# One accumulator per block product in the second feed-forward GEMM, combined once at its end

## Chip, cores and metric

The kernel runs on one core of one Trainium2 chip. The metric is device time in microseconds (us) of one execution. The kernel before has a median of 2658.47 us over 3 runs (2654.43 to 2660.08).

## What is computed

The reference is a chain of four layers in fp32 on 1024 tokens of width 1024: a retention layer, a latent-attention layer, a gated-linear-attention layer and a feed-forward layer with squared ReLU, then a final norm. The change lies in the last part only:

```
def sqrelu_mlp(h, w1, w2):
    return jnp.square(jax.nn.relu(h @ w1)) @ w2
...
        x = x + sqrelu_mlp(rms_norm(x, norm_ffn), w1, w2)
    return rms_norm(x, final_norm)
```

Here w1 is 1024 x 4096 (called FF1 below) and w2 is 4096 x 1024 (FF2).

## The kernel before, in words

All activations are kept transposed (features on the 128 partitions, tokens along the row) as tiles of 128 x 512 fp32: half h is tokens 0 to 511 or 512 to 1023. Every fp32 operand is split into two fp32r parts, a high part made by ScalarE (ACT, a copy) and a low part made by VectorE (DVE, source minus high part); a product is then three matmuls, high by high, high by low and low by high (`mm3`, lines 230 to 232).

The GEMMs are run as 2 x 2 block products in the seven-product form of Strassen and Winograd. The seven products are named 1 to 7 and always come in the order 1, 2, 6, 7, 5, 4, 3 (`FIRST + REST`). Operands of 1, 2 and 3 are blocks as they are; 4, 5, 6 and 7 take sums of blocks. The weight sums are made by GpSimd (POOL) in `W7.sums` (line 638), then split by ACT and DVE (`w_split`, lines 629 and 630). There is room for one set of split weights: a pair of weight tiles is filled again as soon as the two products that read it are done.

**FF1** is 16 jobs of 256 output rows. Each job has 7 products of 12 matmuls of 128 x 512. Class `Fresh` takes the products out of PSUM (line 550 on DVE) and combines them into the four blocks (m, h) of the job. `u_done` applies ReLU, the row norm (line 2096, DVE) and the square (line 2099, ACT) and stores the tile to DRAM: four stores a job.

**FF2** goes over the 32 tiles of 128 rows of u in groups, `FF2_GROUPS = (3, 3, 3, 3, 2, 2)`: a group of k has 2k of these tiles as its inner dimension. For the first five groups, `ff2_operands` loads the group's 4k tiles (2k for each half) from DRAM (tile name `uin`), and `Blocks.add` makes the four operand sums of each k (line 452, two on DVE and one on POOL, and line 463 on POOL) and splits all seven operands (lines 187 and 188). Then it goes over the four column slices s of w2: 7 products of 3k matmuls each, whose results class `Added` adds at once into the four output tiles of the slice, which hold the residual from the start:

```
        def m7(self, ps):
            self.direct(ps, (1, 1), (1, 0))
            self.later(self.two, (1, 0))
```

`direct` is a DVE add from PSUM into the output tile (line 588), `plus` a DVE add of a product to a running sum u (line 597), `later` a POOL add of such a sum into an output tile (line 593). In a slice of a group that makes 7 DVE adds, one ACT copy and 4 POOL adds. The operands of a group are given back product by product in slice s = 3, and only then is there room for the next group's.

The last group (`ff_last`) is run as a plain product, 96 matmuls of 128 x 512 for half 0 and 192 of 128 x 256 for half 1, with the final norm folded in.

SBUF tiles of 128 x 512 come from a pool `slots` whose places are handed out oldest first. PSUM has 8 banks for products, taken in turn. Loads, weights and, at this stage, stores are all issued from SP's queue (lines 119, 122 and 686). The order of the instructions on each engine is set when the program is built: the writing order of the code with some parts marked as of high priority, then arranged by the framework's own timeline.

Of the kernel before, what the change touches and what calls it, by code (L numbers as in the profile page):

```python
# [13 lines left out]
F32 = mybir.dt.float32  # L14
F32R = mybir.dt.float32r
MASK = mybir.dt.uint8
AF = mybir.ActivationFunctionType
ALU = mybir.AluOpType
# [4 lines left out]
P = 128  # L23
QS = lambda nc: (nc.scalar, nc.sync)
T = 1024
HALF = 512
D = 1024
# [11 lines left out]
C_WIDE = 2  # L39
C_WAIT = 16  # L40
C_LAST = 3
C_TAIL = "01 11 21- 02 A 12 22- w0 w1 A 06 B 07 A 05 B w0 w2 04 A 03 B 16 17 B w1 15 14 13 w2 26- 27- 25- a 24- a 23- b"
C_NORM = "NP"
C_DVE = 3
# [37 lines left out]
def tile_kernel(ctx, tc, a, out):  # L82
    nc = tc.nc
# [34 lines left out]
    def store(dst, src):  # L118
        store_q.dma_start(out=dst, in_=src)

    def load(dst, src):
        load_q.dma_start(out=dst, in_=src)
# [1964 lines left out]
    for _ in last:  # L2087
        pass
    x7 = nd.x7


    u_dram = {}

    def u_done(i, m, h, ts):
        (t,) = ts
        nc.vector.scalar_tensor_tensor(
            out=t, in0=t, scalar=0.0, in1=nd.rb[h], op0=ALU.max, op1=ALU.mult
        )
        nc.scalar.activation(out=t, in_=t, func=AF.Square)
        d = dp.tile([P, HALF], F32, name=f"u_{i}_{m}_{h}")  # L2100
        store(d, t)
        slots.put(t)
        u_dram[2 * i + m, h] = d

    def ff1_job(i, early=False):
        w = W7(a["w_ff1"][i], w7p)
# [18 lines left out]

    hd = {}

    def ff2_operands(k, j):
        u7 = Blocks(slots, k)
        for h in range(2):  # L2130
            for i in range(2 * k):
                t = slots.get("uin")
                load(t, u_dram[j + i, h])
                u7.add(i, h, t)
        return u7

    j = 0
    for g, k in enumerate(FF2_GROUPS[:-1]):
        u7 = ff2_operands(k, j)
        j += 2 * k  # L2140
        for s in range(4):
            if g == 0:
                slots.held.update(NORM_TAGS)
                for m, h in ((1, 0), (0, 0), (1, 1), (0, 1)):
                    hd[2 * s + m, h] = slots.get(f"y{2 * s + m}_{h}")
                    load(hd[2 * s + m, h], nd.dram[2 * s + m, h])
                slots.held.clear()
            w = W7(a[f"w_ff2_{g}"][s], w7p)
            w.rest()
            drop = u7.drop if s == 3 else None  # L2150
            Added(plain_product, hd, 2 * s).run(w.w, u7.x, FIRST + REST, drop)

    def ff_last(g, k):
        slots.held.update(NORM_TAGS)
        u = {}
        for h in range(2):
            for i in range(2 * k):
                t = slots.get("uin")
                load(t, u_dram[j + i, h])
                u[i, h] = slots.get("uh", F32R), slots.get("ul", F32R)  # L2160
                split(*u[i, h], t)
                slots.put(t)

        def tiles(w, s, h, cols, norm):
            wh, wl = w
            for m2 in range(2):
                m = 2 * s + m2
                ps = bank8()[:, : cols.stop - cols.start]
                for i in range(2 * k):
                    c = (((1, 0), (2, 3))[m2][i // k] * k + i % k) * P  # L2170
                    c = slice(c, c + P)
                    x = (t[:, cols] for t in u[i, h])
                    mm3(ps, wh[:, c], wl[:, c], *x, i == 0, i == 2 * k - 1)
                tick()
                o = hd[m, h][:, cols]
                with tc.high_priority():
                    nc.vector.tensor_tensor(out=o, in0=ps, in1=o, op=ALU.add)
                norm.add(o)
                g = gain("final_norm_2", m)
                nc.scalar.activation(out=o, in_=o, func=AF.Copy, scale=g)  # L2180

        def done(h, cols, norm, n):
            yield n
            r4 = norm.rstd(pc)
            yield n
            rb = spread(r4, pc, "rbp")
            for m in range(NK):
                o = hd[m, h][:, cols]
                eng = nc.gpsimd if n or m % 3 == 2 else nc.vector
                eng.tensor_tensor(out=o, in0=o, in1=rb, op=ALU.mult)  # L2190
                c = slice(h * HALF + cols.start, h * HALF + cols.stop)
                nc.sync.dma_start(out=out[m * P : (m + 1) * P, c], in_=o)

        ws = {}
        for h, cols in ((0, slice(0, HALF)), (1, slice(0, 256)), (1, slice(256, HALF))):
            last = cols.start > 0
            norm = NormOnTensor(D) if last else Norm(D, (nc.vector,))
            for s in range(4):
                if s not in ws:
                    ws[s] = load_w(a[f"w_ff2_{g}"][s])  # L2200
                tiles(ws[s], s, h, cols, norm)
            defer(done(h, cols, norm, 0 if last else 1))
# [77 lines left out]
def prepare(inp):  # L2280
# [63 lines left out]
    row = 0  # L2344
    for i, k in enumerate(FF2_GROUPS):
        rows = w2[row * P : (row + 2 * k) * P]
        r[f"w_ff2_{i}"] = np.stack([blocks(cut(rows, s, 256), 1) for s in range(4)])
        row += 2 * k
    return r
# [1 line left out]

# [14 lines left out]
```

## Time and profile before

| what | value |
|---|---|
| median of 3 runs | 2658.47 us |
| the profiled execution | 2656.4 us |
| its span, first to last instruction | 2654.6 us |
| mean granted TensorE clock | 0.965 of full speed |
| PE busy | 2480.7 us (93%) |
| DVE busy | 2043.8 us (77%) |
| ACT busy | 1094.7 us (41%) |
| POOL busy | 1322.9 us (50%) |
| DMA, all queues | 305.59 MB, mean 115 GB/s |

PE is TensorE's matmuls and PEld its weight loads; shares are of the span. Matmuls are pipelined, so a busy PE says little about how fast it goes: the number of matmuls in a stretch says more. [...]

### The profile page before, as it was taken

The numbers are of one execution on the slowest core, as the hardware profiler recorded it, in microseconds if no ns is written. First come the engines' busy times: TensorE is split into PE (matmuls) and PEld (weight loads), VectorE is DVE, ScalarE is ACT, GpSimd is POOL, SyncE is SP. The second block draws the span as 40 slices with busy tenths as digits, with TensorE's granted clock in tenths as the row PEclk, the third lists the DMA queues.
The fourth block names the chain that finished last, engine by engine and source line by source line (L and its number), as shares of the span: only waits on it lengthen the run. The fifth ranks groups of instructions, "written<-read, shape, count | busy, mean of one in ns | idle before, by whom it ended". The sixth has DMA issues, their size and how long they took to land. (4 is left out here: it accounts for less than half of the span.)

```text
span 2654.6 us, 35499 instructions
## 1 busy us (share of the span) xinstructions
PE 2480.7 (93%) x12676; PEld 2067.6 (78%) x12676; DVE 2043.8 (77%) x2967; ACT 1094.7 (41%) x1882; POOL 1322.9 (50%) x973
## 2 busy tenths in 40 slices
PE   7999999999997999999998988889999999988888
PEld 5888888877785788888877878777778888766767
DVE  8787787789978835767578677887796676898895
ACT  7323323354443324555444433334553333333334
POOL 4345444435736712222135266865453333888884
PEclk8999999999998999999997989989999999988999
DMA  6523223633333322122342333446333334523322
GB/s 228 161 78 117 105 91 119 211 105 110 105 114 116 101 90 75 58 63 73 120 136 81 109 122 108 138 159 216 123 115 113 106 102 136 162 81 95 91 91 81
DMA packets 141005, 305.59 MB, mean 115 GB/s; under 512 B 16123, under 2 KB 19579, under 8 KB 140828
## 3 DMA queue, kind: packets, MB, share of 16 engines
q1 hardware_dynamic: 118940, 263.47, 31.0%
q10 hardware_dynamic: 21888, 39.86, 4.0%
q8 instruction: 100, 1.64, 0.3%
q14 instruction: 77, 0.63, 0.1%
HBM read 213.08 MB, written 88.08 MB: 113 GB/s over the span
## 5 line engine op out<-in xcount | busy, mean ns | idle before, releaser
L593 POOL TENSOR_TENSOR y<-y,u 128x512 f32<-128x512 f32 x120 | 205.6, 1731 | 75.7 <-DVE y L588 37.2
L629 ACT ACTIVATE wh<-ws 128x1024 fp32r<-128x1024 f32 (+3 forms) x200 | 142.6, 725 | 201.5 <-PE ps L231 106.9
L630 DVE TENSOR_TENSOR wl<-ws,wh 128x1024 fp32r<-128x1024 f32 (+3 forms) x196 | 198.8, 1022 | 22.9 <-ACT wh L629 22.4
L638 POOL TENSOR_TENSOR wsb<-wsc 128x512 f32<-128x512 f32 (+2 forms) x72 | 103.1, 1433 | 218.4 <-issue 137.7
L629 ACT ACTIVATE wh<-wsb 128x1024 fp32r<-128x1024 f32 (+2 forms) x76 | 73.6, 968 | 214.8 <-PE ps L231 134.1
L1428 POOL TENSOR_SCALAR p<-p,rl 128x512 f32<-128x512 f32 (+2 forms) x96 | 61.2, 648 | 194.7 <-DVE rl L1426 93.5
L638 POOL TENSOR_TENSOR ws<-ws,wsb 128x512 f32<-128x512 f32 (+2 forms) x72 | 102.3, 1421 | 96.2 <-DVE wl L630 96.2
L550 DVE TENSOR_TENSOR y<-ps,one 128x512 f32<-128x512 f32 x108 | 73.5, 686 | 93.3 <-PE ps L232 43.8
L550 DVE TENSOR_TENSOR y<-ps,y 128x512 f32<-128x512 f32 x112 | 76.9, 686 | 76.4 <-PE ps L232 50.0
L638 POOL TENSOR_TENSOR wsb<-ws,wsb 128x512 f32<-128x512 f32 (+2 forms) x72 | 111.0, 1542 | 49.1 <-DMA ws<-w_a 40.9
L550 DVE TENSOR_TENSOR one<-ps,one 128x512 f32<-128x512 f32 x168 | 114.3, 683 | 21.0 <-PE ps L232 18.7
L588 DVE TENSOR_TENSOR y<-ps,y 128x512 f32<-128x512 f32 x152 | 99.8, 681 | 30.7 <-POOL y L593 25.7
L630 DVE TENSOR_TENSOR wl<-wsc,wh 128x1024 fp32r<-128x1024 f32 (+2 forms) x76 | 112.3, 1483 | 10.9 <-ACT wh L629 10.2
L231 PE MATMUL ps<-x5l,wh 128*128 128x512 f32 x248 | 101.6, 410 | 11.4 <-DVE x5l L188 8.4
L638 POOL TENSOR_TENSOR wsc<-wsc,ws 128x512 f32<-128x512 f32 (+2 forms) x72 | 111.8, 1553 | 0.0
L230 PE MATMUL ps<-x6h,wh 128*128 128x512 f32 x248 | 102.8, 417 | 7.4 <-ACT wh L629 4.1
L230 PE MATMUL ps<-x1h,wh 128*128 128x512 f32 x248 | 101.5, 410 | 8.7 <-ACT x1h L192 8.0
L230 PE MATMUL ps<-x3h,wh 128*128 128x512 f32 x248 | 102.1, 412 | 7.6 <-DVE y L588 7.6
L230 PE MATMUL ps<-x2h,wh 128*128 128x512 f32 x248 | 102.2, 413 | 5.7 <-ACT wh L629 4.4
L630 DVE TENSOR_TENSOR wl<-wsb,wh 128x1024 fp32r<-128x1024 f32 (+2 forms) x76 | 105.3, 1385 | 2.4 <-ACT wh L629 2.0
L232 PE MATMUL ps<-x5h,wl 128*128 128x512 f32 x248 | 101.2, 408 | 4.0 <-DVE wl L630 4.0
L231 PE MATMUL ps<-x6l,wh 128*128 128x512 f32 x248 | 101.5, 409 | 3.1 <-DVE x6l L188 3.1
(475 smaller groups left out, 8860.4 us busy)
## 6 DMA issues: line engine op xcount, KB each, us to landing
uin<-u SPq DMA_DIRECT2D x64, 256.0 KB, 3.5
u<-y SPq DMA_DIRECT2D x48, 256.0 KB, 2.0
ws<-w_ff SPq DMA_DIRECT2D x23, 512.0 KB, 4.5
ws<-w_a SPq DMA_DIRECT2D x21, 512.0 KB, 5.2
ws<-w_b SPq DMA_DIRECT2D x20, 512.0 KB, 3.3
wsc<-w_a SPq DMA_DIRECT2D x16, 512.0 KB, 4.4
v<-v SPq DMA_DIRECT2D x32, 256.0 KB, 3.6
gate<-g SPq DMA_DIRECT2D x32, 256.0 KB, 3.2
```

Source lines behind the costliest of these rows:

```text
L230: nc.tensor.matmul(ps, lh, rh, start=start, stop=False)
L231: nc.tensor.matmul(ps, lh, rl, start=False, stop=False)
L232: nc.tensor.matmul(ps, ll, rh, start=False, stop=stop)
L550: nc.vector.tensor_tensor(out=o, in0=p, in1=i, op=ALU.add)
L588: nc.vector.tensor_tensor(out=t, in0=ps[0], in1=t, op=ALU.add)
L593: nc.gpsimd.tensor_tensor(out=t, in0=t, in1=u, op=ALU.add)
L629: nc.scalar.activation(out=hi, in_=raw, func=AF.Copy)
L630: lo_eng.tensor_tensor(out=lo, in0=raw, in1=hi.bitcast(F32), op=ALU.subtract)
L638: eng.tensor_tensor(out=o, in0=x, in1=y, op=op)
L1428: nc.gpsimd.tensor_scalar(out=pr, in0=pr, scalar1=rl, scalar2=0.0, op0=ALU.mult, op1=ALU.add)
```

## The change

- In FF1, for the first 14 jobs, the four tiles of a job are kept until the last is squared. Then POOL makes the operand sums from them (`u_sums`, four adds), and seven tiles are stored instead of four. The last two jobs still store their four tiles.
- In FF2, `split_load` loads each of the seven operands of a k ready made, into the place of its low part, and splits it there: 7k loads for a group instead of 4k, and no sums.
- `Sevens` keeps, for each slice s, one SBUF accumulator for each of the seven products over all five groups (28 in all instead of 16 output tiles). A product is one DVE add from PSUM into its accumulator; accumulators 2, 4 and 3 start as residual tiles loaded from DRAM, the other four are filled by an ACT copy in the first group. There are no POOL adds until `close`, which follows each slice of the fifth group and does four adds on DVE and four on POOL.
- Seven more places in the pool (`f_slots`). The scratch for descriptors of DMAs issued from GpSimd is cut to 2048 bytes; this kernel issues none there.
- The rows of w2 are put in another order on the host, so that the pair of tiles of one FF1 job forms the two block rows.

```diff
+F_SLOTS = 7
...
+    fslots = pool(ctx, "f_slots")
+    slots.add(fslots, [f"f{i}" for i in range(F_SLOTS)])
...
+    def u_sums(i):
+        b11, b21, b12, b22 = (u_raw.pop((i, m, h)) for h in range(2) for m in range(2))
+        t1, n6 = slots.get("t1"), slots.get("n6")
+        G = nc.gpsimd
+        G.tensor_tensor(out=t1, in0=b12, in1=b11, op=ALU.subtract)
+        G.tensor_tensor(out=n6, in0=t1, in1=b22, op=ALU.subtract)
+        G.tensor_tensor(out=b12, in0=b12, in1=b22, op=ALU.subtract)
+        keep_u(6, i, n6)
+        G.tensor_tensor(out=n6, in0=b21, in1=n6, op=ALU.add)
+        for n, t in ((1, b11), (2, b21), (7, b12), (5, t1), (4, n6), (3, b22)):
+            keep_u(n, i, t)
+            slots.put(t)
+
+    def keep_u(n, i, t):
+        u_dram[n, i] = dp.tile([P, HALF], F32, name=f"u{n}_{i}")
+        store(u_dram[n, i], t)
...
         nc.scalar.activation(out=t, in_=t, func=AF.Square)
-        d = dp.tile([P, HALF], F32, name=f"u_{i}_{m}_{h}")
-        store(d, t)
-        slots.put(t)
-        u_dram[2 * i + m, h] = d
+        if i >= 16 - FF2_GROUPS[-1]:
+            keep_u((m, h), i, t)
+            slots.put(t)
+            return
+        u_raw[i, m, h] = t
+        if (m, h) == (0, 1):
+            u_sums(i)
...
-    def ff2_operands(k, j):
-        u7 = Blocks(slots, k)
-        for h in range(2):
-            for i in range(2 * k):
-                t = slots.get("uin")
-                load(t, u_dram[j + i, h])
-                u7.add(i, h, t)
-        return u7
+    def split_load(src):
+        lo, hi = slots.get("lo", F32R), slots.get("hi", F32R)
+        raw = lo.bitcast(F32)
+        load(raw, src)
+        split(hi, lo, raw)
+        return hi, lo
+
+    class Sevens:
+        OF = {2: (0, 0), 4: (1, 0), 3: (0, 1)}
...
+        def run(self, w, x, drop):
+            for n in FIRST + REST:
+                if n not in self.acc:
+                    slots.held.update(NORM_TAGS)
+                    self.acc[n] = self.old(*self.OF[n]) if n in self.OF else slots.get("y")
+                    slots.held.clear()
+                    first = n not in self.OF
+                else:
+                    first = False
+                (ps,) = plain_product(w[n], x[n])
+                t = self.acc[n]
+                with tc.high_priority():
+                    if first:
+                        nc.scalar.activation(out=t, in_=ps, func=AF.Copy)
+                    else:
+                        nc.vector.tensor_tensor(out=t, in0=ps, in1=t, op=ALU.add)
+                if drop:
+                    for pair in x[n]:
+                        slots.put(*pair)
+
+        def close(self):
+            a, V, G = self.acc, nc.vector, nc.gpsimd
+            last = self.old(1, 1)
+            for e, o, i in (
+                (V, 2, 1), (G, 6, 1), (V, 7, 6), (G, 6, 5), (V, 4, 7), (V, 5, 7), (G, 3, 6)
+            ):
+                e.tensor_tensor(out=a[o], in0=a[o], in1=a[i], op=ALU.add)
+            G.tensor_tensor(out=a[5], in0=a[5], in1=last, op=ALU.add)
...
+    ys = [Sevens(s) for s in range(4)]
     for g, k in enumerate(FF2_GROUPS[:-1]):
-        u7 = ff2_operands(k, j)
-        j += 2 * k
-        for s in range(4):
...
-            drop = u7.drop if s == 3 else None
-            Added(plain_product, hd, 2 * s).run(w.w, u7.x, FIRST + REST, drop)
+        x = {n: [split_load(u_dram[n, j + i]) for i in range(k)] for n in FIRST + REST}
+        j += k
+        for s, c in enumerate(ys):
+            w = W7(a[f"w_ff2_{g}"][s], w7p)
+            w.rest()
+            c.run(w.w, x, s == 3)
+            if g == len(FF2_GROUPS) - 2:
+                c.close()
...
+        if i < len(FF2_GROUPS) - 1:
+            rows = rows.reshape(k, 2, P, D).transpose(1, 0, 2, 3).reshape(-1, D)
...
-    nc = bacc.Bacc("TRN2", target_bir_lowering=False, num_devices=1)
+    nc = bacc.Bacc("TRN2", target_bir_lowering=False, num_devices=1, dynamic_dma_scratch_size=2048)
```

Ahead of FF1 no engine's order changes, and PE's order in FF1 stays as it was. Two places show what moves. Line numbers are each kernel's own: from line 42 on, those of the changed kernel stand one or more higher.

The first place is DVE at the change from the third group of FF2 to the fourth, in slice s = 3. Before (x5l, x3l, x6l are low parts of operands, uin the loaded tiles, wl low parts of weights, y and u the adds of products):

```order
L188 TENSOR_TENSOR x5l_22358<-uin,x5h_22357 128x512
L188 TENSOR_TENSOR x3l_22378<-uin,x3h_22377 128x512
L597 TENSOR_TENSOR u<-ps_22282,u 128x512
L452 TENSOR_TENSOR uin<-uin 128x512
L188 TENSOR_TENSOR x5l_22365<-uin,x5h_22364 128x512
L630 TENSOR_TENSOR wl<-wsb,wh 128x768
L188 TENSOR_TENSOR x3l_22399<-uin,x3h_22398 128x512
...
L188 TENSOR_TENSOR x5l_22372<-uin,x5h_22371 128x512
...
L630 TENSOR_TENSOR wl<-wsc,wh 128x768
L588 TENSOR_TENSOR y_0_21080<-ps_22296,y_0_21080 128x512
```

And now (lo the low parts of operands, split in place, y the adds of products into accumulators):

```order
L2188 TENSOR_TENSOR y<-ps_22279,y 128x512
L189 TENSOR_TENSOR lo<-lo,hi 128x512
L2188 TENSOR_TENSOR y_0_21255<-ps_22290,y_0_21255 128x512
L631 TENSOR_TENSOR wl<-ws,wh 128x768
...
L2188 TENSOR_TENSOR y<-ps_22301,y 128x512
L189 TENSOR_TENSOR lo<-lo,hi 128x512 x3
L2188 TENSOR_TENSOR y<-ps_22312,y 128x512
...
L2188 TENSOR_TENSOR y<-ps_22323,y 128x512
L631 TENSOR_TENSOR wl<-wsb,wh 128x768
L189 TENSOR_TENSOR lo<-lo,hi 128x512 x2
```

The sums of loaded tiles (uin from uin) are gone from DVE, and the splits now come three at a time between the adds of the products, in the order of the products.

The second place is POOL in the middle of FF1. Before, only the weight sums of the jobs (ws, wsb, wsc are raw weights and their sums):

```order
L638 TENSOR_TENSOR ws_18878<-ws_18878,wsb_18886 128x512
L638 TENSOR_TENSOR wsb_19030<-wsc_19024 128x512
L638 TENSOR_TENSOR wsb_19030<-ws_19022,wsb_19030 128x512
L638 TENSOR_TENSOR wsc_19024<-wsc_19024,ws_19022 128x512
L638 TENSOR_TENSOR ws_19022<-ws_19022,wsb_19030 128x512
```

And now, with the four sums of the job just finished between them (one is the block (0, 1), y the other three blocks, t1 and n6 the two new tiles):

```order
L639 TENSOR_TENSOR wsc_19399<-wsc_19399,ws_19397 128x512
L2102 TENSOR_TENSOR t1_19221<-one_19123,y_19138 128x512
L2103 TENSOR_TENSOR n6_19222<-t1_19221,y_19184 128x512
L2104 TENSOR_TENSOR one_19123<-one_19123,y_19184 128x512
L2106 TENSOR_TENSOR n6_19222<-y_19169,n6_19222 128x512
L639 TENSOR_TENSOR ws_19397<-ws_19397,wsb_19405 128x512
```

The last weight sum (ws) of a later job now stands behind the four sums, and the fourth of these writes a tile that a store still has to read.

## Rows read from the trace of the kernel before

**Rows 1.** Waits of TensorE's weight loads in FF2: us in total, times, longest us
```profile
PEld ps L230 <- DVE y L588: 10.8, 5, 3.4
PEld ps L232 <- DVE wl L630: 10.7, 9, 2.8
PEld ps L231 <- DVE x5l L188: 9.9, 3, 3.8
```

**Rows 2.** PE's instructions in time: last product of FF1, first of FF2, first 256-wide
```profile
2263.46 0.40 PE L230 MATMUL ps<-x3h,wh 128*128 128x512 f32 x1
...
2266.25 0.40 PE L230 MATMUL ps<-x1h,wh 128*128 128x512 f32 x1
...
2615.31 0.29 PE L230 MATMUL ps<-uh,wh 128*128 128x256 f32 x1
```

**Rows 3.** Stretches: length, busy us (count) of PE, PEld, DVE, ACT, POOL; PEclk, DMA share, GB/s
```profile
2000.00:2240.00 240.00, 240.00 (x1033) 193.62 (x1033) 162.59 (x184) 82.95 (x110) 79.05 (x49) 1.00 0.32 109
2266.00:2322.00 56.00, 53.16 (x218) 41.44 (x217) 50.56 (x65) 20.59 (x33) 44.87 (x27) 0.97 0.49 157
2322.00:2392.00 70.00, 62.59 (x249) 48.48 (x248) 62.05 (x71) 26.07 (x41) 60.38 (x39) 0.90 0.29 87
...
2462.00:2532.00 70.00, 63.08 (x262) 49.54 (x261) 62.26 (x72) 26.08 (x41) 61.37 (x39) 0.95 0.28 87
2532.00:2592.00 60.00, 52.71 (x207) 40.09 (x206) 55.73 (x71) 23.55 (x41) 48.15 (x36) 0.94 0.32 98
...
2270.00:2280.00 10.00, 7.31 (x24) 5.21 (x22) 10.00 (x14) 4.42 (x8) 5.97 (x3) 0.83 1.02 374
...
2340.00:2350.00 10.00, 5.43 (x12) 3.18 (x11) 10.00 (x10) 3.52 (x6) 7.99 (x6) 0.50 0.13 40
...
2300.00:2540.00 240.00, 217.33 (x881) 169.73 (x880) 207.93 (x239) 86.65 (x136) 211.38 (x135) 0.93 0.30 90
```

**Rows 4.** Groups of DVE's instructions from 2300 to 2540 us: busy us, mean ns | idle before
```profile
L588 DVE TENSOR_TENSOR y<-ps,y 128x512 f32<-128x512 f32 x70 | 46.0, 682 | 22.7 <-POOL y L593 22.7
...
L630 DVE TENSOR_TENSOR wl<-wsc,wh 128x768 fp32r<-128x768 f32 x14 | 19.9, 1420 | 0.0
...
L597 DVE TENSOR_TENSOR u<-ps,u 128x512 f32<-128x512 f32 x28 | 19.0, 678 | 0.4 <-PE ps L232 0.4
...
L630 DVE TENSOR_TENSOR wl<-ws,wh 128x384 fp32r<-128x384 f32 x14 | 11.2, 801 | 0.0
```

**Rows 5.** DVE's instructions in time, around the fifth group: start us, us
```profile
2531.77 0.55 DVE L630 TENSOR_TENSOR wl<-ws,wh 128x384 fp32r<-128x384 f32 x1
...
2541.10 1.78 DVE L452 TENSOR_TENSOR uin<-uin 128x512 f32<-128x512 f32 x1
...
2592.99 1.21 DVE L144 TENSOR_TENSOR wl<-ws,wh 128x1024 fp32r<-128x1024 f32 x1
2594.12 1.88 DVE L588 TENSOR_TENSOR y<-ps,y 128x512 f32<-128x512 f32 x3
```

**Rows 6.** Groups of POOL's instructions from 2300 to 2540 us
```profile
L593 POOL TENSOR_TENSOR y<-y,u 128x512 f32<-128x512 f32 x58 | 110.4, 1926 | 24.4 <-DVE y L588 21.4 <-ACT wh L629 3.0
...
L638 POOL TENSOR_TENSOR wsb<-wsc 128x384 f32<-128x384 f32 x13 | 16.9, 1301 | 0.2
```

**Rows 7.** All engines in time around the change from one FF1 job to the next
```profile
2216.15 1.29 POOL L638 TENSOR_TENSOR ws<-ws,wsb 128x512 f32<-128x512 f32 x1 [5.23 <-DVE wl L630]
...
2226.93 0.40 PE L232 MATMUL ps<-x3h,wl 128*128 128x512 f32 x1
...
2227.18 0.63 ACT L629 ACTIVATE wh<-ws 128x512 fp32r<-128x512 f32 x1 [1.65 <-PE ps L231]
...
2231.38 0.63 ACT L2099 ACTIVATE one<-one 128x512 f32<-128x512 f32 x1 [1.67 <-DVE one L2096]
```

**Rows 8.** The page's DMA issues: count, size, median us from issue to landing
```profile
uin<-u SPq DMA_DIRECT2D x64, 256.0 KB, 3.5
u<-y SPq DMA_DIRECT2D x48, 256.0 KB, 2.0
```

More of the change, by code (lines that the diff above doesn't have):

```diff
@@ L2089, in tile_kernel @@
     x7 = nd.x7
-    u_dram = {}
+    fslots = pool(ctx, "f_slots")
+    slots.add(fslots, [f"f{i}" for i in range(F_SLOTS)])
+    u_dram, u_raw = {}, {}
+    def u_sums(i):
[13 more added lines that the diff above has]
+        store(u_dram[n, i], t)
     def u_done(i, m, h, ts):
@@ L2126, in tile_kernel, with __init__, old @@
     hd = {}
-    def ff2_operands(k, j):
-        u7 = Blocks(slots, k)
-        for h in range(2):
-            for i in range(2 * k):
-                t = slots.get("uin")
-                load(t, u_dram[j + i, h])
-                u7.add(i, h, t)
-        return u7
+    def split_load(src):
[6 more added lines that the diff above has]
+        OF = {2: (0, 0), 4: (1, 0), 3: (0, 1)}
+        def __init__(self, s):
+            self.s, self.acc = s, {}
+        def old(self, m, h):
+            t = slots.get(f"y{2 * self.s + m}_{h}")
+            load(t, nd.dram[2 * self.s + m, h])
+            return t
+        def run(self, w, x, drop):
[25 more added lines that the diff above has]
+            G.tensor_tensor(out=a[5], in0=a[5], in1=last, op=ALU.add)
+            slots.put(last, a[1], a[6], a[7])
+            for (m, h), n in (((0, 0), 2), ((1, 0), 4), ((0, 1), 3), ((1, 1), 5)):
+                hd[2 * self.s + m, h] = a[n]
@@ L2137, in tile_kernel @@
     j = 0
+    ys = [Sevens(s) for s in range(4)]
     for g, k in enumerate(FF2_GROUPS[:-1]):
-        u7 = ff2_operands(k, j)
-        j += 2 * k
-        for s in range(4):
[L2142 to L2147, printed above, removed]
+        x = {n: [split_load(u_dram[n, j + i]) for i in range(k)] for n in FIRST + REST}
+        j += k
+        for s, c in enumerate(ys):
@@ L2157, in ff_last @@
             for i in range(2 * k):
[L2158 to L2162, printed above, removed]
+                u[i, h] = split_load(u_dram[(i % 2, h), j + i // 2])
         def tiles(w, s, h, cols, norm):
```

## The prediction

> **What bounds the kernel now.** I read the stretches first. In the middle of FF1 (2000 to 2240 us) PE is busy throughout and its clock is full; DVE is busy 68% and POOL 33% of the time [rows 3]. FF1 is bound by PE, and work added there costs nothing as long as DVE and POOL keep up. The pitch of a matmul follows from FF1's last product: 12 matmuls in 2266.25 - 2263.46 = 2.79 us, 0.2325 us each [rows 2] (1033 in 240 us [rows 3] say the same). A job of 84 matmuls takes 19.5 us.
>
> Next FF2. From its first matmul to the first 256-wide one it takes 2615.31 - 2266.25 = 349.1 us [rows 2]. In it stand 28 products x 3 x 14 = 1176 matmuls plus 96 of the last group, 1272, which at 0.2325 us are 295.7 us. So FF2 **loses 53 us**. Where: a stretch of 70 us has room for 301 matmuls and holds 249 or 262 (a third such stretch between them: 244) [rows 3], that is 12, 9 and 13 us lost, each once per group; the first group loses 241 - 218 = 23 matmuls or 5 us, and the fifth group with the start of the last 258 - 207 = 51 or 12 us [rows 3]. Within a group the loss sits where the operands change: 12 matmuls in 10 us, at a clock of 0.50, with DVE busy all the time [rows 3]. TensorE waits there for low parts of operands and weights and for adds that DVE makes [rows 1]. So DVE, at the changes of group, sets the pace, and over a whole stretch it is busy 207.9 of 240 us, POOL 211.4 [rows 3].
>
> Why DVE is that full: an add of two SBUF tiles takes 1.78 us where POOL works beside it, while adds that take one operand from PSUM stay at 0.68 in a mean of 70 and of 28 [rows 4, 5]. Their pitch is 0.60, from three in 1.88 us [rows 5]. I put the pitches of SBUF operations at 0.60 for 512 columns, 0.87 for 768 (an estimate between 0.68 and the 1.21 us of 1024 columns [rows 5], less the 0.08 that durations overlap) and 0.47 for 384 [rows 5]. In the 240 us stretch DVE has 239 instructions [rows 3]: 98 from PSUM [rows 4], 41 of 768 columns (three groups like the one shown, 14, 14 and 13), 14 of 384 [rows 4] and 86 others of 512. Alone they would take 58.8 + 35.7 + 6.6 + 51.6 = 153 us. It takes 208, so 55 us are due to POOL: **0.26 us of DVE for each busy us of POOL**.
>
> [...]
>
> **The change part by part.**
>
> *POOL in FF2.* The 4 adds a slice (1.93 us each [rows 6]) and 2k operand sums a group go: 22 x 1.93 = 42 us for a group of three, the sums put at the same. There remain 16 weight sums of about 1.3 us [rows 6], 21 us. With it DVE's extra falls from 16 us a group (55 us over 240/70 groups) to 0.26 x 21 = 5.5 us.
>
> *DVE in FF2.* 7 adds a slice stay 7. The 6 sums a group go (3.6 us). A group of three now has 49 operations of 0.60, 12 of 0.87, 4 of 0.47: 41.7, with 5.5 extra 47 us. PE needs 252 x 0.2325 = 58.6. So DVE is no longer the bound over a group; at the change of group I count again. From the end of the first product of slice 3 (when the first places come free) DVE must do, ahead of the last split that the next group's first slice needs, 8 adds, 19 splits (two pairs are loaded ahead), three weight splits of 768 and one of 384: 27 x 0.60 + 3.1 = 19.3 us, plus 0.26 x 8 weight sums x 1.3 = 2.7, plus the wait for the first load, 3.5 us [rows 8] and 0.63 for its high part [rows 7]. That is 26.1 us. PE wants it after 12 products of 2.09 us and seven matmuls of the thirteenth, 26.7 us. A tie; in order, with the clock liable to fall whenever PE waits (0.50 above), I charge 3 us for each of three changes, between 0 and 8 (most of what it loses now). Before, DVE had in the same window the sums too, and each at POOL's mercy.
>
> *Loads at the change.* 19 loads of 256 KB instead of 12. The rate of 374 GB/s in 10 us with the DMA engines full [rows 3] is 0.70 us for one: 13.3 us, the last there after some 18 us, ahead of 25. Hidden by the product order. Behind them on SP's queue stand weights for slices 1 and 2, wanted over 10 us later.
>
> *First group.* Its 21 splits and 12 residual tiles are loaded in FF1's last job, which frees 56 places; the change loses 5 us now, I take 2.5 (0 to 6). 16 of its 28 products are taken out by ACT, which is a third busy [rows 3].
>
> *Fifth group, close and last group.* From the end of the first product of slice 3 of the fourth group to the last 512-wide one PE has 54 + 168 + 96 = 318 matmuls, 73.9 us. DVE has 98 operations of 0.60 (16 of them from close), four of 0.33 and four of 1.13: 64.6 us; POOL has 16 small weight sums and 16 adds, some 40 us, which cost DVE 10.4 more, and the first load 4.1: 79 us. So here DVE stays behind, by about 5 us, and its adds and POOL's in close wait for each other. I find no gain: 12 us lost as now (4 to 20).
>
> *FF1.* Each of 14 jobs gets 4 POOL adds and 3 stores. POOL: 79.05 us in 12.3 jobs [rows 3] is 6.4 a job; the adds at the dearest mean seen, 1.93 [rows 6], 7.7, and half a us for the fourth, which waits for a store (2.0 us [rows 8]) that the third covers: 14.6 of 19.5. DVE goes from 13.2 a job [rows 3] to 13.2 + 0.26 x 8.2 = 15.3. What queues behind the adds is the last weight sum. Of a job that ends at E = 2227.16, the last tile is squared by E + 4.85, so that sum ends at 4.85 + 8.2 + 1.3 = E + 14.4; ACT takes it only when its pair of weight tiles is free, which is at the end of a job (2227.18) [rows 7], E + 19.5. 5 us to spare; cost 0. Stores: 0.8 MB more a job, 40 GB/s on top of 109 at a DMA share of 0.32 [rows 3]; they wait for POOL on SP's queue, with nothing due soon behind them. The seven tiles need more places, of which seven are new. Cost 0. The smaller scratch: nothing is issued by GpSimd; 0.
>
> **Sum.** FF2 loses 2.5 + 3 x 3 + 12 = 23.5 us instead of 53.3: 29.8 us less. On the profiled execution, 2656.4 us (2.1 below the median of the runs), that gives **2626.6, say 2627 us**. Its own range: 0 + 0 + 4 = 4 lost to 6 + 24 + 20 = 50; I take 2610 to 2642, and a few us beyond at the lower end.
>
> **Rivals.**
> 1. *DVE stays the bound at the changes of group*: its extra time doesn't fall with POOL's, or the splits, which all lie in one window, come late with the loads. For it: 26.1 against 26.7 is no margin. Against: POOL's work there halves. Each change then loses 8 instead of 3: 2642 us. Chance 0.13.
> 2. *As 1, and close costs as much as it saved*: 16 adds on DVE and 16 on POOL that wait on each other, an extra us each way in the fifth group: 2657, no change. POOL and DVE wait for each other's adds already now (22.7 and 21.4 us [rows 4, 6]). Chance 0.06.
> 3. *FF1 becomes bound by POOL, and the kernel slower*: POOL's job grows past 19.5 us once one of the four adds takes (19.5 - 6.9) / 4 = 3.15 us. At 4 us a job is 3.4 us longer, 14 jobs 48 us: 2627 + 48 = 2675. It decides the sign from 3.8 us on. Against: the dearest group mean is 1.93 [rows 6]. Chance 0.04.
> 4. *Loads one at a time*: 19 loads at 3.5 us [rows 8] are 66 us, 41 more than the 25 in which they are wanted, at four changes: some 2790. Against: the 374 GB/s of [rows 3] can't come about that way. Chance 0.02.
> 5. *The change doesn't do what it says in time*: the program's order gives the freed time back as longer waits at the same places, about 2655. Chance 0.03.
>
> [...]
>
> **How the numbers follow.** The forecast has 0.72. The range 2606 to 2652 holds it with its bounds and rival 1; left out are rivals 2 to 5, some 0.15. Faster by over 0.2% (5.3 us, about what a measurement can tell) are the forecast and rival 1, 0.85; within it rivals 2 and 5, 0.09; slower rivals 3 and 4, 0.06.
>
> **What would show it.** FF1's jobs still at full clock and 0.2325 us a matmul; FF2's first matmul within 2 us of 2266. The group period falls from 70 us to 60 to 63. The 768-column weight splits on DVE fall from 1.42 us [rows 4] to 1.1 or so, POOL's busy time from 2300 to 2540 by half. The stretch of 12 matmuls in 10 us is gone. The prediction is wrong if a group still takes 66 us or more (rivals 1, 4), if a matmul pitch or a wait appears in FF1 (rival 3), or if the time from the fifth group to the first 256-wide matmul grows by over 10 us (rival 2).

## The result and the profile after

The changed kernel takes **2610.0 us** (median of 4 runs, 2609.0 to 2618.5), the kernel before 2658.0 beside it: a ratio of **0.9828, 95% interval 0.9805 to 0.9851**. The profiled execution took 2610.9 us (span 2609.0), 45.5 less than that of before. Forecast were 2627 us, a range of 2606 to 2652 and a gain of 29.8; the time lies in the range, at its lower end.

PE's instructions in time, around FF2's first matmul and the first 256-wide one:

```profile
2268.18 0.40 PE L233 MATMUL ps<-x3h,wl 128*128 128x512 f32 x1
2268.41 0.40 PE L231 MATMUL ps<-hi,wh 128*128 128x512 f32 x1
...
2569.17 0.40 PE L233 MATMUL ps<-hi,wl 128*128 128x512 f32 x1
2569.40 0.28 PE L231 MATMUL ps<-hi,wh 128*128 128x256 f32 x1
```

FF2 takes 2569.40 - 2268.41 = 301.0 us instead of 349.1 [rows 2], against 295.7 for its matmuls at their pitch: it loses 5.3 us instead of 53.4. So 48.1 us come from FF2; 2.2 us go again because FF2 starts that much later. The stretches (columns as in [rows 3]): the middle of FF1, then one for each of FF2's first four groups, one for the fifth group with the last, and the 240 us of FF2 that [rows 3] has of before:

```profile
2000.00:2240.00 240.00, 240.00 (x1033) 193.68 (x1032) 186.90 (x188) 84.66 (x113) 153.16 (x99) 1.00 0.44 153
2268.00:2328.00 60.00, 58.81 (x252) 46.90 (x251) 40.09 (x52) 31.19 (x53) 22.56 (x16) 1.00 0.60 207
2328.00:2387.00 59.00, 59.00 (x254) 47.55 (x254) 47.20 (x64) 23.68 (x39) 19.91 (x16) 1.00 0.45 147
2387.00:2446.00 59.00, 59.00 (x255) 47.68 (x254) 48.63 (x68) 24.39 (x39) 21.68 (x16) 1.00 0.45 152
2446.00:2504.00 58.00, 58.00 (x251) 46.79 (x250) 48.05 (x67) 24.16 (x40) 19.85 (x16) 1.00 0.42 141
2504.00:2570.00 66.00, 63.86 (x274) 50.36 (x273) 63.91 (x87) 23.73 (x39) 42.80 (x28) 1.00 0.26 85
2300.00:2540.00 240.00, 240.00 (x1033) 193.56 (x1031) 195.36 (x268) 99.05 (x160) 97.56 (x75) 1.00 0.44 146
```

From the second group to the fourth PE has no gap and its clock stays full (PEclk 1.00: the share of full speed that was granted); a group takes 58 to 59 us where it took 70. DVE is busy 47 to 49 us of one, POOL 20 to 22 instead of 60 to 61. In 2300 to 2540 us PE does 1033 matmuls instead of 881 [rows 3]. What still loses time is the first group and the fifth with the last. The waits of TensorE's weight loads in FF2, of which [rows 1] are the like of before:

```profile
PEld ps L233 <- DVE wl L145: 1.8, 2, 1.0
PEld ps L231 <- DVE y L2188: 1.6, 1, 1.6
PEld ps L231 <- ACT hi L188: 1.2, 1, 1.2
PEld ps L233 <- DVE wl L631: 1.2, 2, 0.8
```

The waits of 10 us each for DVE's adds, its weight parts and its operand parts are gone. DVE's groups from 2300 to 2540 us, as [rows 4]:

```profile
L2188 DVE TENSOR_TENSOR y<-ps,y 128x512 f32<-128x512 f32 x109 | 73.5, 684 | 28.1 <-PE ps L233 28.1
L189 DVE TENSOR_TENSOR lo<-lo,hi 128x512 fp32r<-128x512 f32 x83 | 59.9, 750 | 11.2 <-ACT hi L188 11.1
L631 DVE TENSOR_TENSOR wl<-wsc,wh 128x768 fp32r<-128x768 f32 x13 | 17.4, 1342 | 0.3 <-ACT wh L630 0.3
...
L631 DVE TENSOR_TENSOR wl<-wsb,wh 128x768 fp32r<-128x768 f32 x13 | 12.4, 955 | 5.4 <-ACT wh L630 5.4
```

In front of the adds DVE now waits for PE (28.1 us), where it had waited for POOL (22.7). An add from PSUM takes what it took, 684 ns against 682.

For all kernels below I give what FF2 lost **by place**, from the same count: PE's 512-wide matmuls in order of start, cut into groups of 252, 252, 252, 252, 168 and 96, each group's time less 0.2325 us a matmul. All 1272 stand in each trace; where the timeline view merges two of one line into a row, marked x2, they count as two. The last column is what follows FF2's last 512-wide matmul, to the end of the span; 256-wide matmuls done ahead of it (9, 5 and 14 in three of the kernels) are counted there, at 0.117 us each.

| kernel | FF2 us | lost | first group | three changes | fifth + last | after FF2 |
|---|---|---|---|---|---|---|
| before | 349.1 | 53.4 | 5.6 | 35.6 | 12.2 | 39.3 |
| changed | 301.0 | 5.3 | 1.8 | 0.2 | 3.3 | 39.6 |
| sums alone | 315.1 | 19.4 | 1.8 | 13.3 | 4.3 | 40.6 |
| accumulators alone | 329.6 | 33.9 | 2.0 | 18.9 | 12.9 | 40.7 |
| accumulators, no sums | 299.6 | 3.9 | 0.0 | 0.3 | 3.6 | 39.0 |
| places alone | 354.8 | 59.1 | 6.2 | 41.2 | 11.6 | 38.8 |
| three places | 303.3 | 7.5 | 0.1 | 0.3 | 7.1 | 39.2 |
| four POOL adds put back | 314.9 | 19.1 | 4.0 | 6.4 | 8.7 | 51.8 |
| two POOL adds put back | 312.4 | 16.6 | 2.8 | 1.5 | 12.4 | 41.1 |
| close on DVE | 299.3 | 3.5 | 2.0 | 0.2 | 1.4 | 43.8 |
| last low parts on POOL | 301.2 | 5.5 | 1.5 | 0.2 | 3.8 | 45.1 |
| three POOL adds in FF1 | 306.6 | 10.8 | 6.5 | 0.2 | 4.2 | 39.0 |

### The profile page after: what moved, and what is told of

It reads as the page before. It is cut to its first block, busy times and chain, and to the rows that moved or that the text cites. A ratio compares the mean times of both kernels' runs of the same rounds, so it can differ in the third digit from the quotient of the medians.

```text
span 2609.0 us, 35559 instructions
## 1 busy us (share of the span) xinstructions
PE 2463.3 (94%) x12676; PEld 2062.0 (79%) x12676; DVE 2003.3 (77%) x2939; ACT 1090.6 (42%) x1878; POOL 1247.8 (48%) x937
## 5 line engine op out<-in xcount | busy, mean ns | idle before, releaser
L631 DVE TENSOR_TENSOR wl<-ws,wh 128x1024 fp32r<-128x1024 f32 (+3 forms) x196 | 207.9, 1068 | 23.5 <-ACT wh L630 22.5
L231 PE MATMUL ps<-hi,wh 128*128 128x512 f32 (+1 forms) x488 | 185.7, 381 | 2.0 <-DVE y L2188 1.2
L232 PE MATMUL ps<-lo,wh 128*128 128x512 f32 (+1 forms) x488 | 185.4, 380 | 0.0
L233 PE MATMUL ps<-hi,wl 128*128 128x512 f32 (+1 forms) x488 | 183.6, 381 | 1.4 <-DVE wl L145 1.0
L551 DVE TENSOR_TENSOR y<-ps,y 128x512 f32<-128x512 f32 x112 | 77.0, 687 | 73.9 <-PE ps L233 47.3
L551 DVE TENSOR_TENSOR y<-ps,one 128x512 f32<-128x512 f32 x108 | 73.5, 686 | 76.9 <-PE ps L233 27.8
L551 DVE TENSOR_TENSOR one<-ps,one 128x512 f32<-128x512 f32 x168 | 114.2, 682 | 15.9 <-PE ps L233 12.5
L631 DVE TENSOR_TENSOR wl<-wsc,wh 128x1024 fp32r<-128x1024 f32 (+2 forms) x76 | 109.3, 1443 | 10.4 <-ACT wh L630 9.7
L231 PEld LDWEIGHTS ps<-hi,wh 128*128 128x128 f32 x488 | 91.7, 188 | 22.0 <-DVE y L2188 1.6
L233 PEld LDWEIGHTS ps<-hi,wl 128*128 128x128 f32 x488 | 91.7, 188 | 21.8 <-DVE wl L145 1.8
L631 DVE TENSOR_TENSOR wl<-wsb,wh 128x1024 fp32r<-128x1024 f32 (+2 forms) x76 | 98.1, 1291 | 12.6 <-ACT wh L630 12.2
L232 PEld LDWEIGHTS ps<-lo,wh 128*128 128x128 f32 x488 | 91.7, 188 | 18.9
L2188 DVE TENSOR_TENSOR y<-ps,y 128x512 f32<-128x512 f32 x124 | 83.5, 684 | 29.3 <-PE ps L233 29.1
L630 ACT ACTIVATE wh<-wsc 128x1024 fp32r<-128x1024 f32 (+2 forms) x76 | 73.1, 968 | 58.4 <-PE ps L232 48.1
L189 DVE TENSOR_TENSOR lo<-lo,hi 128x512 fp32r<-128x512 f32 x106 | 77.9, 762 | 21.1 <-ACT hi L188 20.9
```

The lines of the kernel that those rows point to most:

```text
L189: (lo_eng or nc.vector).tensor_tensor(out=lo, in0=src, in1=hi.bitcast(F32), op=ALU.subtract)
L231: nc.tensor.matmul(ps, lh, rh, start=start, stop=False)
L232: nc.tensor.matmul(ps, lh, rl, start=False, stop=False)
L233: nc.tensor.matmul(ps, ll, rh, start=False, stop=stop)
L551: nc.vector.tensor_tensor(out=o, in0=p, in1=i, op=ALU.add)
L630: nc.scalar.activation(out=hi, in_=raw, func=AF.Copy)
```

## The experiments

The change has two parts, operand sums made in FF1 and one accumulator per product, and a side condition, seven places more. The first four runs take them apart; the two with one part alone have the seven places too.

**Sums alone.** The changed kernel with FF2's adds as before:

```diff
-    class Sevens:
...
-            c.run(w.w, x, s == 3)
...
+            Added(plain_product, hd, 2 * s).run(w.w, x, FIRST + REST, drop)
```

> The operand sums are made in FF1 and stored, as in the change, but FF2 adds into the 16 output tiles as before, so POOL keeps its 4 adds a slice (31 us of the 42 us a group that the change takes from it). Theory A (the gain of 47 us is POOL's time taken out of FF2, which slowed DVE): a quarter of the gain, about 2646 us. Theory B (the gain is that no sum stands between load and split at the change of group): nearly all of it, 2610 to 2616 us. Theory C (either part alone brings DVE under PE's 58.6 us a group, so either alone brings most): 2612 to 2625 us here and in the run with accumulators alone.

Measured: 2627.5 us (2625.1 to 2631.0), ratio 0.9888, interval 0.9863 to 0.9912: 30.3 us gained.

**Accumulators alone.** The kernel before with the class `Sevens`, and its operand sums left in FF2:

```diff
+    ys = [Sevens(s) for s in range(4)]
...
-            Added(plain_product, hd, 2 * s).run(w.w, u7.x, FIRST + REST, drop)
+            c.run(w.w, u7.x, s == 3)
+            if g == len(FF2_GROUPS) - 2:
+                c.close()
```

> FF2 keeps one accumulator per product and combines at the end, as in the change, but the operand sums stay in FF2 at the change of group, as before (12 loads, three sums on DVE and three on POOL in place of every 4 loads more). Theory A: three quarters of the gain, about 2622 us. Theory B: little, 2645 to 2657 us, with TensorE still waiting for operand splits at every change of group. Theory C: 2612 to 2625 us.

Measured: 2638.3 us (2633.5 to 2642.3), ratio 0.9924, interval 0.9900 to 0.9948: 19.5 us gained. None of the three theories gives this pair. A and B each wanted one part to carry the gain, C either part to bring most; but 30.3 and 19.5 add up to 49.8, about the whole 48.0. In FF2 it is much the same: 34.0 and 19.5 us, somewhat more than the 48.1 of both. The sums weigh more, and the table says where: with the accumulators alone the fifth group and the last still lose 12.9 us, with the sums alone 4.3. What TensorE's weight loads wait for most in FF2 of the accumulators-alone run:

```profile
PEld ps L233 <- DVE wl L631: 8.1, 13, 1.0
PEld ps L232 <- DVE x6l L189: 6.6, 5, 3.0
PEld ps L232 <- DVE x5l L189: 4.5, 3, 1.9
```

The low parts of sums are two of the three. In the sums-alone run weight parts are nearly all that is left, 19.6 us of them:

```profile
PEld ps L233 <- DVE wl L631: 19.6, 17, 3.9
```

**Places alone.** The kernel before with the seven places and the smaller scratch:

```diff
+F_SLOTS = 7
...
+    fslots = pool(ctx, "f_slots")
+    slots.add(fslots, [f"f{i}" for i in range(F_SLOTS)])
...
+    nc = bacc.Bacc("TRN2", target_bir_lowering=False, num_devices=1, dynamic_dma_scratch_size=2048)
```

> The kernel before with the seven places more and the smaller scratch, nothing else. Theories A, B and C: no change, 2653 to 2662 us. Rival P (what helps is that more operands can be loaded ahead): 2635 us or less.

Measured: 2662.7 us, 10 runs from 2658.0 to 2666.2, ratio 1.0017, interval 1.0006 to 1.0028. Rival P falls; the places and the smaller scratch by themselves cost some 5 us (5.7 in FF2's own time; in the two traces it stands at the third change of group, which loses 16.0 us instead of 9.6).

**Three places.** The changed kernel with `F_SLOTS = 3`:

```diff
-F_SLOTS = 7
+F_SLOTS = 3
```

> The changed kernel with three new places instead of seven, so that a group of three and the 28 accumulators fill all 70 and nothing of the next group is loaded before the first product of slice 3 is done. If DVE is only just quick enough at the change of group, as the forecast's 26.1 against 26.7 us has it, two more splits and one exposed load of 3.5 to 5 us at each of four changes cost 2 to 6 us each: 2618 to 2634 us. If there is room to spare: 2609 to 2614 us.

Measured: 2611.9 us (2606.8 to 2620.0), no different from the changed kernel. FF2 takes some 2 us more in this trace, but none of it at the changes of group, which lose 0.3 together against 0.2; it stands in the fifth group and the last (7.1 against 3.3). So loading ahead is not what makes the change of group fast. It hardly takes place in the changed kernel either: in its SP queue one load of the second group goes out at 2315.00, 1.2 us ahead of the end of the first product of slice 3 (2316.2), and 20 behind it:

```profile
2315.00 0.33 SPq L123 DMA_DIRECT2D lo<-u  x1
...
2316.58 12.99 SPq L123 DMA_DIRECT2D lo<-u  x20
```

**No sums.** What do operand sums cost where they stood, their time or their place in the chain from load to split? The accumulators-alone run with its sums left out:

```diff
+                if not self.sums:
+                    return
...
-                G.tensor_tensor(out=b11, in0=t, in1=b11, op=ALU.subtract)
+                if self.sums:
+                    G.tensor_tensor(out=b11, in0=t, in1=b11, op=ALU.subtract)
```

> The run with accumulators alone (FF2 329.4 us), with its operand sums left out: products 6, 7, 5 and 4 are made with the low and high parts of plain blocks, so the numbers are not those of the reference. Loads (12 a group of three), their order and the 21 splits stay. Theory S (what the sums cost at the change of group is their time: 9 on DVE at 0.60 us, 9 on POOL at 1.93 us and 0.26 us of DVE each: 9.9 us a change): FF2 301 to 306 us, 2610 to 2617 us. Theory L (it is the chain of load, sum and split, or the order of the loads, with all of the upper half's blocks first, so that a first product's operands wait for several loads): FF2 313 us or more, 2621 us or more.

Measured: 2606.1 us (2602.9 to 2609.6); FF2 299.6 us:

```profile
2263.49 0.39 PE L231 MATMUL ps<-x1h,wh 128*128 128x512 f32 x1
...
2563.13 0.28 PE L231 MATMUL ps<-uh,wh 128*128 128x256 f32 x1
```

FF2 is 30 us shorter than with the sums and as short as in the changed kernel, with the old loads in their old order. Theory L's loads and their order fall. Theory S is the nearer, though the run is a little faster than its ranges: it counted 9.9 us of DVE a change, 0.6 of them to spare, and the sums had cost 6.2 a change and some 9 in the fifth group and the last. One part of theory L isn't tested: where a sum is left out, its split no longer waits for it either. The traces speak for time. In front of the splits of operands, from 2328 to 2520 us, DVE waits in the accumulators-alone run (the first three lines, 5.1 us) no more than in the changed kernel (the fourth):

```profile
DVE x5l L189 <- ACT x5h L188: 2.8, 3, 1.4
DVE x1l L189 <- ACT x1h L188: 1.5, 3, 0.7
DVE x2l L189 <- ACT x2h L188: 0.8, 2, 0.5
```

```profile
DVE lo L189 <- ACT hi L188: 7.2, 6, 2.4
```

So making the sums in FF1 does not gain by seven ready-made loads; that it gains by taking the sums' time out of the changes of group is what the count and these waits say, short of a run that keeps the one and drops the other.

**Four POOL adds put back.** What do POOL's adds cost, their time or the waits of DVE and POOL for each other? In the changed kernel POOL does as many adds at the same places, into a tile that nobody reads:

```diff
                         nc.vector.tensor_tensor(out=t, in0=ps, in1=t, op=ALU.add)
+                    for _ in range({2: 1, 7: 1, 5: 2}.get(n, 0)):
+                        nc.gpsimd.tensor_tensor(out=spin[0], in0=spin[1], in1=t, op=ALU.add)
...
+    spin = [stage("spin") for _ in range(2)]
```

> The changed kernel with four POOL adds a slice put back at the places where the kernel before has them, as many columns wide, each reading the accumulator just added to and writing a scratch tile that nobody reads. POOL's queue and time are those of the run with the sums alone, but no add of DVE waits for one of POOL's. That run's FF2 took 315.1 us against 301.0. Theory D (what the POOL adds cost is their time: 0.26 us of DVE for each busy us of POOL, and the weight sums queued behind them): 8 adds of 1.93 us in the window at each of four changes of group, 4.0 us more of DVE there with 0.6 us to spare, 14 us in all: FF2 313 to 318 us, 2621 to 2629 us. Theory E (the cost is the hand-over: DVE's add waits for POOL's on the same tile): FF2 300 to 304 us, 2608 to 2614 us.

Measured: 2635.3 us (2626.4 to 2638.3); FF2 314.9 us, in theory D's range and the same as with the sums alone, 315.1; the time is above D's range. But the two agree in the sum only. At the three changes these adds lose 6.4 us where the sums-alone run loses 13.3; the rest comes in the first group and in the fifth with the last. The groups of DVE's operand splits in 2328 to 2520 us, in the changed kernel, then with the sums alone, then with the adds put back:

```profile
L189 DVE TENSOR_TENSOR lo<-lo,hi 128x512 fp32r<-128x512 f32 x74 | 53.1, 747 | 7.3 <-ACT hi L188 7.2
```

```profile
L189 DVE TENSOR_TENSOR lo<-lo,hi 128x512 fp32r<-128x512 f32 x69 | 61.8, 932 | 9.9 <-ACT hi L188 9.9
```

```profile
L189 DVE TENSOR_TENSOR lo<-lo,hi 128x512 fp32r<-128x512 f32 x68 | 61.7, 941 | 7.0 <-ACT hi L188 7.0
```

Beside POOL's adds a split takes 0.19 us more, whoever reads what they write. What DVE waits for in the same stretch, with the sums alone and with the adds put back:

```profile
DVE y L589 <- POOL y L594: 16.8, 14, 1.2
```

```profile
DVE y L2188 <- PE ps L233: 12.1, 12, 1.4
```

The 16.8 us in which DVE stands and waits for POOL's add on the same output tile are in the one and not in the other. So at the changes of group the time that POOL's adds take from DVE costs about half of what they cost (6.2 of 13.1 us over the changed kernel); the other half, by the difference of the two runs, is put down to the hand-over, which theory E named. Behind FF2 the adds put back cost 12 us more. One wait of 10 us stands there; POOL's last add of close starts only at 2589.48, behind the added ones, against 2560.23 in the changed kernel:

```profile
PE ps_stat L274 <- DVE acc L266: 10.0, 1, 10.0
```

**Two POOL adds put back**, to see whether there is room for some (the edit is against the run with four):

```diff
-                    for _ in range({2: 1, 7: 1, 5: 2}.get(n, 0)):
+                    for _ in range({2: 1, 5: 1}.get(n, 0)):
```

> The run with four POOL adds a slice put back (FF2 314.9 us, against 301.0 without), with two a slice instead of four. By the forecast's count of the change of group (26.1 us of DVE against 26.7 of PE): 4 adds in the window cost DVE 2.0 us, 0.6 of it spare, 1.4 us at each of four changes: FF2 305 to 308 us. If there were room for all of it, and the four adds cost by another way (weight sums late in POOL's queue): 301 to 303 us. If the cost were simply proportional: 308 us.

Measured: 2624.9 us (2621.4 to 2628.2), FF2 312.4 us: none of the three. By place it is clearer: the three changes lose 1.5 us, 1.3 over the changed kernel (forecast 4.2), and with four adds 6.2 over it (forecast 10.2). Against adds that by the price of 0.26 cost DVE 2.0 and 4.0 us a change, that is 0.4 and 2.1 lost: an estimated 1.6 to 1.9 us to spare, not 0.6. Most of the rest, 9 us, is lost in the fifth group, where DVE has nothing to spare; the stretches from 2520 us on (columns as above):

```profile
2520.00:2540.00 20.00, 17.41 (x66) 13.04 (x66) 20.00 (x26) 3.84 (x7) 14.96 (x12) 0.91 0.09 26
2540.00:2560.00 20.00, 16.39 (x64) 11.94 (x63) 20.00 (x23) 3.16 (x5) 18.19 (x13) 0.94 0.11 41
2560.00:2580.00 20.00, 19.21 (x80) 14.91 (x79) 20.00 (x22) 5.48 (x8) 17.10 (x9) 0.98 0.28 79
```

Its 8 adds there are 14 us of POOL at the 1.77 us that they take, an estimated 3.8 us of DVE; the other 5 are perhaps close's adds that stand behind them, which no run separates.

**Close on DVE.** The last 3 us, and perhaps a better version:

```diff
-            a, V, G = self.acc, nc.vector, nc.gpsimd
+            a, V, G = self.acc, nc.vector, nc.vector
```

> The changed kernel with all eight adds of each close on DVE, POOL having none. In 2540 to 2560 us, where the changed kernel loses about 3 us, DVE is busy throughout. If the price of POOL's adds is 0.26 us of DVE for each of their us, 16 adds of 2.0 us cost DVE 8.3 us and take 9.6 (16 x 0.60) if DVE does them: no change, 2608 to 2613 us. If the waits of the two engines for each other in close are what costs: up to 3 us less, 2605 to 2609 us. If DVE simply gets fuller: 5 us more or so, 2613 to 2618 us.

Measured: 2610.7 us (2603.3 to 2613.4), no different. From 2540 to 2560 us, the changed kernel and this one:

```profile
2540.00:2560.00 20.00, 17.86 (x73) 13.30 (x73) 20.00 (x26) 4.01 (x5) 11.74 (x7) 1.00 0.27 80
```

```profile
2540.00:2560.00 20.00, 19.05 (x86) 15.08 (x86) 20.00 (x32) 7.04 (x9) 0.00 (x0) 1.00 0.28 79
```

DVE does 32 instructions instead of 26 in the same 20 us once POOL is silent, and FF2 gets 1.7 us shorter; what follows FF2 gets 4 longer in this trace. That agrees with the price of 0.26 us for each us of POOL, by which both ways cost DVE the same; the changed kernel's own runs differ by more than the 3 us in question.

**Last low parts on POOL.**

```diff
-        nc.vector.tensor_tensor(out=wl, in0=ws, in1=wh.bitcast(F32), op=ALU.subtract)
+        lo_eng.tensor_tensor(out=wl, in0=ws, in1=wh.bitcast(F32), op=ALU.subtract)
...
-                    ws[s] = load_w(a[f"w_ff2_{g}"][s])
+                    ws[s] = load_w(a[f"w_ff2_{g}"][s], lo_eng=nc.gpsimd)
```

> The changed kernel with the low parts of the last group's four weight tiles (1024 columns, 1.21 to 1.94 us each on DVE) made on POOL. If DVE's fullness in the fifth group is what loses the last 3 us: 2605 to 2609 us. If TensorE's start on the last group waits for these low parts, which POOL makes slower (an estimated 3 to 4 us for 1024 columns, twice its 1.93 us for 512) and behind close's adds: 2613 to 2622 us.

Measured: 2612.7 us (2605.6 to 2619.0): between the two forecasts, not told from the changed kernel, and no gain. In this trace FF2 keeps its 301.2 us and what follows it gets 5.5 longer. Neither of the last two runs beats the changed kernel; with 5.3 us left to lose in FF2, little was to be had.

**Three POOL adds more in FF1**, for the rival in which FF1 becomes bound by POOL:

```diff
         G.tensor_tensor(out=n6, in0=b21, in1=n6, op=ALU.add)
+        for t in (b11, b21, b22):
+            G.tensor_tensor(out=spin[0], in0=spin[1], in1=t, op=ALU.add)
...
```

> The changed kernel with three POOL adds of the same width more in each of FF1's 14 jobs that make sums (reading tiles of the job, writing a scratch tile that nobody reads). POOL's busy time a job goes from 12.5 us (153.2 in 240) to about 18.2 of 19.5. The forecast gave the last weight sum 5 us to spare behind four adds at 8.2 us. If that count is right: 0.8 us a job late, up to 11 us more, 2612 to 2622 us, with waits of TensorE for weights in FF1. If POOL only has to stay under 19.5 us a job, as its queue can run ahead into the next: no change, 2608 to 2614 us.

Measured: 2620.4 us (2619.0 to 2625.6), 10 us more: the time of the first reading, but not by its way. From 2000 to 2220 us:

```profile
2000.00:2220.00 220.00, 220.00 (x948) 177.53 (x947) 197.54 (x171) 73.98 (x101) 219.22 (x129) 1.00 0.46 154
```

POOL is busy 219.2 of 220 us, and PE doesn't wait: no weight comes late for eleven jobs. The bill comes at FF1's end (its last two jobs take 43.1 us by PE's rows instead of 39.1) and in FF2's first group (6.5 us lost instead of 1.8). There, between 2225 and 2300 us, TensorE waits 8.8 us for weight low parts, against 0.8 in the changed kernel:

```profile
PEld ps L233 <- DVE wl L631: 8.8, 5, 3.5
```

POOL did not fall behind from job to job: the last weight sum of a job starts at 2038.79 and, ten jobs on, at 2226.10, every 18.7 us against the 19.5 of PE's job. One add later POOL stands idle for 5.4 us, and the next weight sum starts at 2234.02, 5.3 us later than in the changed kernel (the last line):

```profile
2038.79 1.28 POOL L639 TENSOR_TENSOR ws<-ws,wsb 128x512 f32<-128x512 f32 x1
...
2226.10 1.29 POOL L639 TENSOR_TENSOR ws<-ws,wsb 128x512 f32<-128x512 f32 x1
...
2234.02 1.63 POOL L639 TENSOR_TENSOR wsb<-wsc 128x512 f32<-128x512 f32 x1 [5.39 <-issue]
```

```profile
2228.77 1.63 POOL L639 TENSOR_TENSOR wsb<-wsc 128x512 f32<-128x512 f32 x1 [6.23 <-issue]
```

So the second reading was right about the jobs, whose work fits, and wrong about the time. What POOL waited for at the end the profile doesn't name ("issue"), and why the adds make FF1's last weights late stays open.

## Why the prediction was right, and where its size was off

**What bound the kernel: right.** DVE at the changes of group, kept there by POOL. With both parts of its load gone, the loss there is 0.2 instead of 35.6 us.

**The price of POOL: right.** In 2300 to 2540 us DVE has 268 instructions: 212 of 512 columns, 39 of 768, 14 of 384 and 3 of 256, at the forecast's pitches (0.33 for the last) 127.2 + 33.9 + 6.6 + 1.0 = 168.7 us. It is busy 195.4, so 26.7 us stand against 97.6 us of POOL: 0.27 each, where 0.26 was forecast. In FF1 it is (186.90 - 162.59 - 4 x 0.60) / (153.16 - 79.05) = 0.30. In these runs the splits, with two SBUF inputs, pay it, and the adds from PSUM don't. From 2328 to 2520 us a split takes 747 ns in the changed kernel and 941 with four POOL adds put back, an add from PSUM 685 and 680:

```profile
L2188 DVE TENSOR_TENSOR y<-ps,y 128x512 f32<-128x512 f32 x94 | 63.5, 685 | 24.4 <-PE ps L233 24.4
```

```profile
L2188 DVE TENSOR_TENSOR y<-ps,y 128x512 f32<-128x512 f32 x87 | 58.1, 680 | 12.5 <-PE ps L233 12.1
```

What makes the two kinds differ no run shows. One reading was off: the 1.78 us for an add of two SBUF tiles is the dearest of 28 such adds, whose median is 0.93; nothing in the sum uses it.

**POOL and DVE in FF2: right.** POOL's busy time fell from 211.4 to 97.6 (forecast: by half), DVE's to 47 or 49 us a group (forecast 47). The 768-wide weight parts fell from 1.42 us to 1.34 for the kind of [rows 4], and to 0.95 for the others (forecast 1.1).

**The three changes of group: mis-sized by 8.8 us.** The step "A tie; in order, with the clock liable to fall whenever PE waits (0.50 above), I charge 3 us for each of three changes" failed; they cost 0.2 together. The count under it stood. DVE's instructions at the change to the second group:

```profile
2319.14 0.69 DVE L189 TENSOR_TENSOR lo<-lo,hi 128x512 fp32r<-128x512 f32 x1 [3.01 <-ACT hi L188]
...
2342.75 0.90 DVE L189 TENSOR_TENSOR lo<-lo,hi 128x512 fp32r<-128x512 f32 x1
...
2352.05 0.69 DVE L2188 TENSOR_TENSOR y<-ps,y 128x512 f32<-128x512 f32 x1 [0.39 <-PE ps L233]
```

PE's first matmul with a low part behind that last split:

```profile
2343.69 0.40 PE L232 MATMUL ps<-lo,wh 128*128 128x512 f32 x1
```

From the end of the first product of slice 3, 2316.2, to the end of the last split, 2343.65, are 27.4 us; 26.1 were forecast with 19 splits and it does all 21 here, 1.2 more. 26.7 us after 2316.2 PE was forecast to want that low part, while it was being made; PE's rows have no gap there. A tie, then, cost nothing, and the clock, 0.90 and 0.95 in these groups before [rows 3], was granted in full (1.00). No row gave the 3 us. By the runs with POOL adds put back there was even an estimated 1.6 to 1.9 us to spare.

**The fifth group, close and the last group: mis-sized by 8.7 us.** The step "I find no gain: 12 us lost as now" set aside its own sum, 79 us of DVE against 73.9 of PE, which gives 5. Lost were 3.3. From 2492.5 to 2569.4 us DVE is busy 73.5 us of 76.9, with 101 instructions:

```profile
2492.50:2569.40 76.90, 74.76 (x318) 59.02 (x317) 73.46 (x101) 31.19 (x51) 43.98 (x29) 1.00 0.37 126
```

That is as full as forecast, only the sum was set aside: the forecast had 106 instructions and 75.0 us for them (64.6 + 10.4), and 4.1 for a first load. The 12 us of before were the fifth group's operand sums: without them, in the run with the sums alone, 4.3 are lost, and with them, in the run with the accumulators alone, 12.9.

**The first group: right** (1.8, forecast 2.5).

**FF1 at no cost: right.** PE does 1033 matmuls in 240 us as before, at full clock (1.00); POOL is busy 12.5 us a job (forecast 14.6), DVE 15.2 (15.3). FF2's first matmul is 2.2 us later, "within 2" missed by little, and hardly by FF1's sums: FF1's first matmul is already 1.5 us later (the first line is before), and FF1's last 14 jobs take 273.6 us by PE's rows in both kernels.

```profile
1945.57 0.40 PE L230 MATMUL ps<-x1h,wh 128*128 128x512 f32 x1
```

```profile
1947.07 0.40 PE L231 MATMUL ps<-x1h,wh 128*128 128x512 f32 x1
```

**The rivals.** 1 and 2 (DVE stays the bound; close gives it back) fell with the 0.2 and 3.3 us. 3 (POOL binds FF1): POOL is busy 12.5 us a job of 19.5; at 19.4, with three more adds, the kernel is 10 us slower, and no run shows where in between that starts. (In the working of rival 3 the sign turns at 3.7 us an add, not at 3.8: 29.8 us over 14 jobs are 2.1 a job.) 4 (loads one at a time): of a change's 21 loads 20 went out in 13 us, and their last split ended 27 us after the first places came free. So they overlap, as [rows 3] had shown: one after another, 21 loads at the 3.5 us of [rows 8] would have taken an estimated 73.5 us. From issue to landing a load now takes a median of 5.1 us, longer than the 3.5 of [rows 8]; the profile page's DMA issues:

```profile
lo<-u SPq DMA_DIRECT2D x98, 256.0 KB, 5.1
```

Without the 3 us charges, and with 5 us for the last part as counted, the sum would have been 2.5 + 0 + 5 = 7.5 us lost and 2610.6 us; measured in the profile are 5.3 lost, and 2610.9 us. As it stood the sum had 23.5 us lost, 18 too many, and the time lies at the very edge of the 2610 to 2642 that the forecast took for itself: the mechanism was right, the size was not.

## What to carry to other kernels

A gap at every change of operands is a count: what must the slower engine do between the moment places come free and the moment TensorE wants the last piece, the time that its neighbour takes from it included (here 0.26 to 0.30 us of DVE for each busy us of POOL). Work made where the neighbour idles (here sums in FF1, with POOL a third busy) cost nothing measurable; with POOL nearly full (219.2 of 220 us) it cost 10 us, and the bill came late, at the stage's end and behind it. When a count comes out as a tie, forecast the tie: a charge for caution is a bias, and a term set "as now" against one's own sum is another.

## What the runs showed of the hardware that was not expected

- The time that DVE loses to POOL is nearly one price in very different mixes, an estimate by pitches of 0.60, 0.87 and 0.47 us: 0.26 us for each busy us of POOL in FF2 before, 0.27 after, 0.30 in FF1; and 16 adds moved from POOL to DVE in close left the total where it was.
- POOL busy 219.2 of 220 us kept TensorE waiting for nothing; the delay of 10 us showed only at FF1's end and in FF2's first group.
- Seven more places for tiles, with the smaller scratch, and nothing else made the kernel before slower, ratio 1.0017 (1.0006 to 1.0028). Why was not tried; the places change which tile waits for which.
